# Five orders for the sixteen matmuls of a weight chunk, and one split buffer moved by 32 bytes

## The chip, the cores and the metric

The kernel runs on one core of a Trainium2 chip. The metric is the device time of one execution in microseconds. The engines named below are TensorE (PE, with its weight loads PEld), VectorE (DVE), ScalarE (ACT), GpSimd (POOL) and SyncE (SP), whose queue issues the loads of weights.

## What is computed

Two layers of a bidirectional encoder, on 256 positions of width 2048, in float32. The first layer mixes by multi-scale pooling and grouped-query attention, the second by an mLSTM with 8 heads of 256, and each ends in a gated MLP of width 5632 with a convolution over three positions:

```python
def reference(x, ...):
    for layer in range(DEPTH):
        h = rms_norm(x, norm_mix[layer])
        if layer % 2 == 0:
            proj = h @ w_in_ab[e]            # pooling | q | k | v
            ...
            mixed = jnp.concatenate([pool_out, att_out], axis=-1) @ w_out_ab[e]
        else:
            mixed = mlstm_mixer(h, w_in_c[o], b_gate_c[o], h_norm_c[o], w_out_c[o])
        x = x + mixed
        x = x + conv_ffn(rms_norm(x, norm_ffn[layer]), w_up[layer], conv_w[layer], conv_b[layer], w_down[layer])
    return x

def conv_ffn(x, w_up, conv_w, conv_b, w_down):
    u = x @ w_up
    ...
    gate, val = jnp.split(u, 2, axis=-1)
    return (jax.nn.silu(gate) * val) @ w_down
```

## The kernel before

Nearly all the work is products of activations with weights. Each float32 factor is split into a high half, rounded to the format that TensorE takes (`F32R`), and a low half, the rest; a product is then high by high, high by low and low by high.

**Weights.** They come in 818 chunks of 128 x 1024 floats, in one fixed order, through the class `Stream`. `load` issues the DMA of a chunk into a raw buffer `w`. `split` writes the high half with ScalarE (line 112) and the low half with VectorE (line 113) into one split buffer `hl` of shape 128 x 2 x 1024: `hl[:, 0]` is the high half, `hl[:, 1]` the low one. `next` hands TensorE the next chunk and runs loads and splits a few chunks ahead. There are four split buffers, in the pool `spool`; within a feed-forward layer `self.more` adds a fifth in a pool of its own (`fh0`, `fh1`), and `home` sends every chunk whose number leaves 4 when divided by 5 there.

**Two ways to multiply.** In `mov_part` and `mov_group` the activations are stationary and a chunk's weights stream past them, 512 columns to a matmul, 12 matmuls a chunk. (The tiles `dn`, `op`, `mo`, `mv`, `qproj`, `kproj`, `vproj`; the quads of the feed-forward layer, tile `p`, have 6 a chunk.) In `stat_part` the weights are stationary. A chunk then holds four row tiles (i = 0 to 3) of 128 rows by two column tiles (m = 0, 1), and each of its eight 128 x 128 blocks is loaded twice: the high block takes a matmul of 512 columns (high and low activations of 256 positions side by side, `src[:, 0:2, :]`), the low block one of 256 columns (high activations alone). These are the 16 matmuls of a chunk. They add up in PSUM: `ps[:, m]` is one bank, whose first half takes high by high and whose second half the two cross terms. `stat_group` uses it for `pool` in the attention layer and `mq`, `mk` in the mLSTM; `up` in the feed-forward layer calls `stat_part` for one chunk at a time, four to a tile f.

**Order.** TensorE's instructions stand in the order in which the program writes them (`manual_schedule`). `wv.tick` lets other work in between every four matmuls: transposes (`tr`, `xt`, `atr`), and attention products of 256 columns (`sc`, `ov`, `qk`, `av`). VectorE's and ScalarE's instructions are put in order by a scheduler that simulates the program. In the mLSTM, `head` transposes a matrix into `atr`, splits it into `at` (ScalarE line 819, VectorE line 820) and multiplies it (`av`); `scaled` evicts and scales `mq` and `mk`. In the feed-forward layer `gather` (lines 391 and 392) evicts an `up` tile, line 936 scales it by the row factors `R`, and `tail` does the rest. There are two PSUM tiles `mm` for the large products.

Of the kernel before, what the change touches and what calls it, by code (L numbers as in the profile page):

```python
# [10 lines left out]
F32R = mybir.dt.float32r  # L11
# [5 lines left out]
P = 128  # L17
D = 2048
S = 256
KT = D // P  # L20
# [9 lines left out]
MD = 256  # L30
# [3 lines left out]
CH = 8  # L34
# [27 lines left out]
NC_ML = M_BG + 1  # L62


class Stream:


# [38 lines left out]
    def split(self, then=None):  # L106
        i = self.n_split
        self.sums(i)
        w, n, width = self.w.pop(i)[:3]
        hl = self.home(i, False).tile([P, 2, CH * P], F32R, tag="hl", name=f"hl{i}")  # L110
        for c in range(0, width, n):
            (self.nc.vector.tensor_copy if i + c == 0 else self.nc.scalar.copy)(hl[:, 0, c : c + n], w[:, c : c + n])  # L112
            self.nc.vector.tensor_sub(hl[:, 1, c : c + n], w[:, c : c + n], hl[:, 0, c : c + n].bitcast(F32))  # L113
            then and then(c // n)
        self.hl[i] = hl
        self.n_split += 1
        self.sums(i + 1)
# [63 lines left out]
def trunk(ctx: ExitStack, tc: tile.TileContext, gx, xT, xn, call, catt, cml, weights, out):  # L181
    nc = tc.nc
    v, a, g, pe = nc.vector, nc.scalar, nc.gpsimd, nc.tensor
# [19 lines left out]
    st = Stream(tc, wp, sp, weights, 5, 2)  # L203
# [3 lines left out]
    first = ExitStack()  # L207
# [10 lines left out]
    wv = Weave()  # L218
# [7 lines left out]
    def mm(out_, lhsT, rhs, start, stop):  # L226
        pe.matmul(out_, lhsT, rhs, start=start, stop=stop, skip_group_check=True)  # L227
# [96 lines left out]
            v.tensor_copy(R, pr[:, 0:S])  # L324
            self.R = R

    def stat_group(act, kts, name):

        ps = mmp.tile([P, 2, 2, S], F32, tag="mm", name=name)
        stat_part(ps, act, kts, True, True)  # L330
        return ps

    def stat_part(ps, act, kts, first, last):

        n = len(kts)
        hl = None
        for i, k in enumerate(kts):
            if i % 4 == 0:
                hl = st.next()
            src = act(k)  # L340
            c = (i % 4) * 2 * P
            for m in range(2):
                mm(ps[:, m].rearrange("p a b -> p (a b)"), hl[:, 0, c + m * P : c + m * P + P],
                   src.rearrange("p a b -> p (a b)"), first and i == 0, False)
            for m in range(2):
                mm(ps[:, m, 1, :], hl[:, 1, c + m * P : c + m * P + P], src[:, 0, :], False,
                   last and i == n - 1)
            wv.tick(0.645)

    def mov_part(ps, act, kts, first, last):  # L350

# [36 lines left out]
    def gather(tp, ps, name):  # L388

        tb = tp.tile([P, 2, S], F32, tag="tb", name=f"tb_{name}")  # L390
        a.copy(tb, ps[:, :, 1, :])  # L391
        v.tensor_add(tb, ps[:, :, 0, :], tb)  # L392
        return tb

    def bc(ap, n):
        return ap.unsqueeze(1).to_broadcast([ap.shape[0], n, ap.shape[1]])
# [23 lines left out]
    def attention_layer(norm, nxt):  # L420
        with ExitStack() as es:
# [180 lines left out]
            def pool_group(ps, g2):  # L602
                if g2 == 0:
                    pw = tp.tile([P, 4, P], F32, tag="rot", name="pw")
                    a.dma_start(pw.rearrange("p g d -> p (g d)"), catt[:, A_PW : A_PW + 512])
                    inv = tp.tile([P, 4, S], F32, tag="rot", name="inv")
                    a.dma_start(inv.rearrange("p g d -> p (g d)"), catt[:, A_INV:])
                    pool_c.extend((pw, inv))
                pw, inv = pool_c
                u = gather(tp, ps, f"pool{g2}")  # L610
                v.tensor_mul(u, u, bc(norm.R, 2))
                yield 0.6
                pad = tp.tile([P, 2, S + 16], F32, tag="q0", name=f"pad{g2}")
                for j in range(2):
                    gi = 2 * g2 + j
                    w = WINDOWS[gi]

                    eng = (g, v)[j]
                    eng.memset(pad[:, j, 0:8], 0.0)
                    eng.memset(pad[:, j, 8 + S : S + 16], 0.0)  # L620
                    eng.tensor_copy(pad[:, j, 8 : 8 + S], u[:, j, :])
                    n, ln = 1, S + 16
                    cur = pad[:, j, :]
                    while n < w:
                        nx = t1p.tile([P, S + 16], F32, tag=(f"w{j}", f"qt2{j}")[n.bit_length() % 2],
                                      name=f"w{gi}_{n}")
                        ln -= n
                        eng.tensor_add(nx[:, :ln], cur[:, :ln], cur[:, n : n + ln])
                        cur, n = nx, 2 * n
                    o = 8 - w // 2  # L630
                    eng.tensor_mul(pad[:, j, :S], cur[:, o : o + S], inv[:, gi])
                    eng.tensor_sub(pad[:, j, :S], pad[:, j, :S], u[:, j, :])
                    yield 0.6
                yield 5.0
                py = psp.tile([P, 2, S], F32, tag="ps", name=f"py{g2}")
                for j in range(2):
                    mm(py[:, j, :], pw[:, 2 * g2 + j, :], pad[:, j, :S], True, True)
                for j in range(2):
                    c = cat(2 * g2 + j)
                    scale = cst[:, C_PSC + 2 * g2 + j : C_PSC + 2 * g2 + j + 1]  # L640
                    a.activation(c[:, 0, :], py[:, j, :], AF.Copy, scale=scale)
                    v.scalar_tensor_tensor(c[:, 1, :], py[:, j, :], scale, c[:, 0, :].bitcast(F32),
                                           ALU.mult, ALU.subtract)
                done.add(f"pool{g2}")
# [13 lines left out]
            ps = mov_group(xx, "kproj", 512, ahead, tables)  # L658
# [5 lines left out]
            with tc.manual_schedule(engines={mybir.EngineType.SP}):  # L664
                ps = mov_group(xx, "qproj0", after=squares)
            wv.add(q_block(ps, 0, 5.5))
            ps = mov_group(xx, "vproj")
# [12 lines left out]
                wv.add(q_block(mov_group(xx, f"qproj{qb}"), qb, (5.0, 4.5)[qb - 1]))  # L680
            pool_c = []
            for g2 in range(2):
                wv.add(pool_group(stat_group(xx, list(range(KT)), f"pool{g2}"), g2))
            need = [set(range(8)), {"pool0", "pool1"}, set(range(8, 12))]

            def ready(i):
# [5 lines left out]
    def mlstm_layer(norm, nxt):  # L692
        with ExitStack() as es:
# [69 lines left out]
            def scaled(ps, name, scale):  # L763
                u = gather(tp, ps, name)
                v.scalar_tensor_tensor(u, u, scale, bc(norm.R, 2), ALU.mult, ALU.mult)
                r = tp.tile([P, 2, 2, S], F32R, tag=name[0] + "hl", name=f"hl_{name}")
                a.copy(r[:, 0], u)
                v.tensor_sub(r[:, 1], u, r[:, 0].bitcast(F32))
                return r
# [3 lines left out]
            low = kc[:, M_MSK + P : M_MSK + 2 * P]  # L773
# [94 lines left out]
            for hp in range(MH // 2):  # L868
                vf = t1p.tile([P, 2, 512], F32, tag="vf", name=f"mvf{hp}")
                for c, n in ((0, MD + 32), (MD, MD)) if hp == 0 else ((0, 512),):  # L870
                    ps = mov_group(xx, f"mv{hp}_{c}", n)
                    if hp + c == 0:
                        wv.until(lambda: norm.rcol is not None)
                        wv.add(gates(ps))
                    n = min(n, 512 if hp else MD)
                    for t in range(2):
                        a.activation(vf[:, t, c : c + n], ps[:, t, :n], AF.Copy, scale=norm.rcol[:, t : t + 1])
                vt = t1p.tile([P, 2, 2, 512], F32R, tag="vt", name=f"mvt{hp}")
                a.copy(vt[:, 0], vf)
                v.tensor_sub(vt[:, 1], vf, vt[:, 0].bitcast(F32))  # L880
                if hp == 0:
                    nrcol = kp.tile([P, 2], F32, tag="nrcol", name="nrcol")
                    v.tensor_scalar_mul(nrcol, norm.rcol, -1.0)
                for hh in range(2):
                    h = 2 * hp + hh
                    q = scaled(stat_group(xx, list(range(KT)), f"mq{h}"), f"q{h}", MD ** -0.5)
                    kk = scaled(stat_group(xx, list(range(KT)), f"mk{h}"), f"k{h}", 1.0)
                    wv.add(head(h, q, kk, vt, hh))
                wv.add(gated(mov_group(xx, f"mo{hp}"), [2 * hp, 2 * hp + 1]))

# [6 lines left out]
    def ffn_layer(layer, norm, nxt):  # L897
        with ExitStack() as es:
# [29 lines left out]
            def up(f, gt, i):  # L928
                ps = mmp.tile([P, 2, 2, S], F32, tag="mm", name=f"up{layer}_{f}")
                for q in range(KT // 4):  # L930
                    stat_part(ps, xx, list(range(4 * q, 4 * q + 4)), q == 0, q == KT // 4 - 1)
                    if q < KT // 4 - 1:
                        yield
                wv.until(lambda: norm.R is not None)
                u = gather(tp, ps, f"up{layer}_{f}")
                v.tensor_mul(u, u, bc(norm.R, 2))  # L936
                tail(u, f, gt, i)
# [167 lines left out]
            for step in _ffn_plan():  # L1105
                kind, c = step[:2]
                if kind != "d" and c not in gts:
                    gts[c] = actp.tile([P, 8, 2, S], F32R, tag=f"B{c % 2}", name=f"g{layer}_{c}")
                key = step[:3]
# [251 lines left out]
```

## Time and profile before

| what | value |
|---|---|
| median of three runs | 2188.6 us (2188.59 to 2188.68) |
| the profiled execution | 2188.64 us |
| its span, first to last instruction | 2186.3 us |
| TensorE busy, matmuls | 2180.1 us, 11328 |
| VectorE busy | 1673.3 us |
| ScalarE busy | 1229.4 us |
| read from HBM | 436.74 MB, 201 GB/s over the span |

The time outside the span is 2.3 us. [...] How far two matmuls stand apart is seen in the chain of waits, which goes back from the last instruction and gives each piece of it by start, length and count.

### The profile page before, as it was taken

The page shows a single profiled execution, that of the slowest core. Times are in us where ns is not written, and L with a number is a line of the kernel's source. Part 1 is how long each engine was busy: PE and PEld are TensorE (multiplying, and loading weights), DVE is VectorE, ACT ScalarE, POOL GpSimd, SP SyncE. Part 2 cuts the span into 40 slices and gives each one's busy share as a digit, 9 for nine tenths or more (in the row PEclk, how much of TensorE's full clock was granted, in tenths as well). Part 3 has the DMA queues.
Part 4 walks back from the last instruction along what each step waited for, and adds up shares of the span by engine and source line. Part 5 has one row for each costly group of instructions (what it writes and reads, how often), then busy time and mean ns, then how long its engine had stood idle before and what let it go on. Part 6 is the DMA issues. An engine that isn't in the chain of part 4 may idle for free.

```text
span 2186.3 us, 30347 instructions
## 1 busy us (share of the span) xinstructions
PE 2180.1 (100%) x11328; PEld 1861.1 (85%) x11328; DVE 1673.3 (77%) x2378; ACT 1229.4 (56%) x1744; POOL 29.2 (1%) x40
## 2 busy tenths in 40 slices
PE   9999999999999999999999999999999999999999
PEld 7888888888888888889888888888888888888887
DVE  7686798878887786666767676679987888778664
ACT  7665565656555565556555554556565655556552
POOL 0020000000000000000000000000000000000000
PEclk9999999999999999999999999999999999999999
DMA  9555557675676755557565555655677667676563
GB/s 323 181 168 174 183 186 231 229 230 195 229 226 221 226 195 192 186 161 205 160 202 179 181 179 176 196 183 181 233 231 226 198 220 233 221 222 196 193 189 125
DMA packets 124950, 440.88 MB, mean 202 GB/s; under 512 B 13850, under 2 KB 16194, under 8 KB 124802
## 3 DMA queue, kind: packets, MB, share of 16 engines
q1 hardware_dynamic: 121568, 434.93, 61.4%
q10 hardware_dynamic: 3074, 3.75, 0.8%
q8 instruction: 89, 1.46, 0.3%
q14 instruction: 59, 0.48, 0.1%
q0 software_dynamic: 160, 0.26, 0.0%
HBM read 436.74 MB, written 2.14 MB: 201 GB/s over the span
## 4 chain that ended last, share of the span: by engine, by line
PE 97%; DVE 2%; issue 0%; ACT 0%
PE up L227 34%; PE dn L227 21%; PE op L227 8%; PE p L227 7%; PE mv L227 4%; PE mq L227 4%; PE mk L227 4%; PE mo L227 4%; PE qproj L227 3%; PE pool L227 1%; PE kproj L227 1%; PE vproj L227 1%; DVE hl L113 1%; PE av L227 1%; PE qk L227 1%; PE end L227 0%
## 5 line engine op out<-in xcount | busy, mean ns | idle before, releaser
L113 DVE TENSOR_TENSOR hl<-w,hl 128x1024 fp32r<-128x1024 f32 (+1 forms) x820 | 992.6, 1218 | 357.6 <-ACT hl L112 350.8
L112 ACT CAST hl<-w 128x1024 fp32r<-128x1024 f32 (+1 forms) x819 | 852.4, 1048 | 662.1 <-PE up L227 137.3
L227 PE MATMUL up<-xx,hl 128*128 128x512 f32 (+1 forms) x4608 | 823.1, 337 | 0.0
L227 PEld LDWEIGHTS up<-xx,hl 128*128 128x128 f32 x4608 | 716.1, 188 | 109.1
L227 PE MATMUL dn<-hl,g 128*128 128x512 f32 x2064 | 480.9, 390 | 0.0
L227 PEld LDWEIGHTS dn<-hl,g 128*128 128x128 f32 x2064 | 385.0, 188 | 78.5
L227 PE MATMUL p<-hl,sx 128*128 128x512 f32 x384 | 103.5, 391 | 1.1 <-DVE hl L113 1.1
L391 ACT COPY tb_up<-up 128x512 f32<-128x512 f32 x72 | 42.2, 587 | 99.4 <-PE up L227 94.8
L917 ACT ACTIVATE y<-tb_up,cst 128x256 f32<-128x256 f32 x144 | 78.8, 595 | 32.6 <-DVE tb_up L936 30.4
L227 PE MATMUL mk<-xx,hl 128*128 128x512 f32 (+1 forms) x512 | 92.2, 338 | 0.0
L227 PE MATMUL mq<-xx,hl 128*128 128x512 f32 (+1 forms) x512 | 92.2, 337 | 0.0
L227 PE MATMUL mv<-hl,xx 128*128 128x512 f32 (+2 forms) x480 | 91.7, 350 | 0.0
L227 PE MATMUL op<-hl,cat 128*128 128x512 f32 x384 | 91.6, 393 | 0.0
L227 PE MATMUL mo<-hl,xx 128*128 128x512 f32 x384 | 90.5, 391 | 0.0
L227 PE MATMUL op<-hl,mcat 128*128 128x512 f32 x384 | 89.5, 392 | 0.0
L227 PEld LDWEIGHTS mq<-xx,hl 128*128 128x128 f32 x512 | 79.3, 188 | 11.6
L227 PEld LDWEIGHTS mk<-xx,hl 128*128 128x128 f32 x512 | 79.1, 188 | 11.4
L227 PEld LDWEIGHTS mv<-hl,xx 128*128 128x128 f32 x480 | 78.3, 189 | 11.2
L392 DVE TENSOR_TENSOR tb_up<-up,tb_up 128x512 f32<-128x512 f32 x72 | 49.8, 692 | 47.7 <-ACT tb_up L391 47.6
L227 PEld LDWEIGHTS op<-hl,mcat 128*128 128x128 f32 x384 | 71.5, 188 | 14.6
L227 PEld LDWEIGHTS mo<-hl,xx 128*128 128x128 f32 x384 | 71.0, 188 | 14.3
L227 PEld LDWEIGHTS op<-hl,cat 128*128 128x128 f32 x384 | 70.9, 188 | 14.1
(240 smaller groups left out, 1740.2 us busy)
## 6 DMA issues: line engine op xcount, KB each, us to landing
w<-in_up SPq DMA_DIRECT2D x288, 512.0 KB, 4.2
w<-in_dn SPq DMA_DIRECT2D x176, 512.0 KB, 4.2
w<-in_m_in SPq DMA_DIRECT2D x124, 512.0 KB, 4.1
w<-in_q SPq DMA_DIRECT2D x112, 512.0 KB, 4.0
w<-in_a_in SPq DMA_DIRECT2D x46, 512.0 KB, 4.4
w<-in_a_out SPq DMA_DIRECT2D x32, 512.0 KB, 3.4
w<-in_m_out SPq DMA_DIRECT2D x32, 512.0 KB, 3.4
w<-in_m_g SPq DMA_DIRECT2D x5, 432.0 KB, 3.5
```

Of the source, the lines that this page charges most:

```text
L112: (self.nc.vector.tensor_copy if i + c == 0 else self.nc.scalar.copy)(hl[:, 0, c : c + n], w[:, c : c + n])
L113: self.nc.vector.tensor_sub(hl[:, 1, c : c + n], w[:, c : c + n], hl[:, 0, c : c + n].bitcast(F32))
L227: pe.matmul(out_, lhsT, rhs, start=start, stop=stop, skip_group_check=True)
L391: a.copy(tb, ps[:, :, 1, :])
L392: v.tensor_add(tb, ps[:, :, 0, :], tb)
L917: a.activation(y[:, j, :], u[:, j, :], AF.Identity, scale=cw(tl, 1), bias=cw(tl, 3))
```

## The change

In `stat_part` the 16 matmuls of a chunk are taken from a table, `ORDERS`, of five orders; in each triple i is the row tile, m the column tile and `low` the half. A caller names the order. Order 0 takes two row tiles at a time, their four high blocks and then their four low ones. Order 1 takes all eight high blocks, row tile by row tile, and then all eight low ones. Order 2 does so too, but goes through the four row tiles of one column tile before the other. Order 3 takes column tile 0, four high and four low, and then column tile 1. Order 4 is that of before: per row tile two high and two low. `pool` has order 3; `mq` and `mk` have 2 and 3 in turn; `up` has f modulo 5. `wv.tick` still comes after every fourth matmul. In `split`, the fifth buffer's tile is 64 floats longer, and the chunk begins 8 floats (32 bytes) into it.

```diff
+def _orders():
+
+    one = [(i, m, low) for i in range(4) for low in range(2) for m in range(2)]
+    return [sorted(one, key=key) for key in (
+        lambda e: (e[0] // 2, e[2]), lambda e: e[2], lambda e: (e[2], e[1]), lambda e: (e[1], e[2]))] + [one]
+
+
+ORDERS = _orders()
...
-        hl = self.home(i, False).tile([P, 2, CH * P], F32R, tag="hl", name=f"hl{i}")
+        home = self.home(i, False)
+        if home is self.spool:
+            hl = home.tile([P, 2, CH * P], F32R, tag="hl", name=f"hl{i}")
+        else:
+            hl = home.tile([P, 2 * CH * P + 64], F32R, tag="hl", name=f"hl{i}")
+            hl = hl[:, 8 : 8 + 2 * CH * P].rearrange("p (a b) -> p a b", a=2)
...
-    def stat_part(ps, act, kts, first, last):
+    def stat_part(ps, act, kts, first, last, order):
...
-        for i, k in enumerate(kts):
-            if i % 4 == 0:
-                hl = st.next()
-            src = act(k)
-            c = (i % 4) * 2 * P
-            for m in range(2):
-                mm(ps[:, m].rearrange("p a b -> p (a b)"), hl[:, 0, c + m * P : c + m * P + P],
-                   src.rearrange("p a b -> p (a b)"), first and i == 0, False)
-            for m in range(2):
-                mm(ps[:, m, 1, :], hl[:, 1, c + m * P : c + m * P + P], src[:, 0, :], False,
-                   last and i == n - 1)
-            wv.tick(0.645)
+        for c in range(0, n, 4):
+            hl = st.next()
+            src = [act(k) for k in kts[c : c + 4]]
+            for at, (i, m, low) in enumerate(ORDERS[order]):
+                w = hl[:, low, (2 * i + m) * P : (2 * i + m + 1) * P]
+                if low:
+                    mm(ps[:, m, 1, :], w, src[i][:, 0, :], False, last and c + i == n - 1)
+                else:
+                    mm(ps[:, m].rearrange("p a b -> p (a b)"), w, src[i].rearrange("p a b -> p (a b)"),
+                       first and c + i == 0, False)
+                if at % 4 == 3:
+                    wv.tick(0.645)
...
-                wv.add(pool_group(stat_group(xx, list(range(KT)), f"pool{g2}"), g2))
+                wv.add(pool_group(stat_group(xx, list(range(KT)), f"pool{g2}", 3), g2))
...
-                    q = scaled(stat_group(xx, list(range(KT)), f"mq{h}"), f"q{h}", MD ** -0.5)
-                    kk = scaled(stat_group(xx, list(range(KT)), f"mk{h}"), f"k{h}", 1.0)
+                    q = scaled(stat_group(xx, list(range(KT)), f"mq{h}", 2 + h % 2), f"q{h}", MD ** -0.5)
+                    kk = scaled(stat_group(xx, list(range(KT)), f"mk{h}", 3 - h % 2), f"k{h}", 1.0)
...
-                    stat_part(ps, xx, list(range(4 * q, 4 * q + 4)), q == 0, q == KT // 4 - 1)
+                    stat_part(ps, xx, list(range(4 * q, 4 * q + 4)), q == 0, q == KT // 4 - 1, f % len(ORDERS))
```

How the instructions move is shown at two places. The first is TensorE in the mLSTM, head 0, from the last chunk of `mq` (`hl_8945`) into the first chunk of `mk` (`hl_8966`); each row is an instruction's line, operation, output and inputs, the size of its output and how often it stands there in succession. 128x512 are high blocks, 128x256 low ones; `cols` is a small product that a tick lets in. Before:

```order
L227 MATMUL mq_8921<-xx_2399,hl_8945 128x512 x2
L227 MATMUL mq_8921<-xx_2399,hl_8945 128x256 x2
L227 MATMUL cols<-cst,rows_b 128x40 x4
L227 MATMUL mq_8921<-xx_2399,hl_8945 128x512 x2
L227 MATMUL mq_8921<-xx_2399,hl_8945 128x256 x2
L227 MATMUL mk_9027<-xx_2399,hl_8966 128x512 x2
L227 MATMUL mk_9027<-xx_2399,hl_8966 128x256 x2
```

and with the change:

```order
L242 MATMUL mq_8921<-xx_2399,hl_8945 128x512 x8
L242 MATMUL mq_8921<-xx_2399,hl_8945 128x256 x4
L242 MATMUL cols<-cst,rows_b 128x40 x4
L242 MATMUL mq_8921<-xx_2399,hl_8945 128x256 x4
L242 MATMUL mk_9027<-xx_2399,hl_8966 128x512 x4
L242 MATMUL mk_9027<-xx_2399,hl_8966 128x256 x4
```

The pairs of two long and two short matmuls have become eight and eight in `mq` (order 2) and four and four in `mk` (order 3).

The second place is VectorE in the mLSTM, head 0, where `at` is split for the product `av`; `tb_q` is the evicted `mq` of the next head, `A` and `arg` are the head's matrices, `hl` the split of weights. Before:

```order
L788 SCALAR_TENSOR_TENSOR arg_9390<-G_9387,mc,kml 128x128
L392 TENSOR_TENSOR tb_q_9240<-mq_9119,tb_q_9240 128x512
L113 TENSOR_TENSOR hl_9279<-w_9171,hl_9279 128x1024
L820 TENSOR_TENSOR at_9266<-atr_9261,at_9266 128x512
L765 SCALAR_TENSOR_TENSOR tb_q_9240<-tb_q_9240,R_8741 128x512
```

and with the change:

```order
L802 SCALAR_TENSOR_TENSOR arg_9390<-G_9387,mc,kml 128x128
L406 TENSOR_TENSOR tb_q_9240<-mq_9119,tb_q_9240 128x512
L128 TENSOR_TENSOR hl_9279<-w_9171,hl_9279 128x1024
L779 SCALAR_TENSOR_TENSOR tb_q_9240<-tb_q_9240,R_8741 128x512
L834 TENSOR_TENSOR at_9266<-atr_9261,at_9266 128x512
```

`at` now stands behind the scaling of `tb_q`; the same holds for heads 2, 4 and 6. On ScalarE, `at`'s high half (`CAST at<-atr`) stands behind the exponential `ACTIVATE arg<-arg` at the same four places, where it stood ahead of it. Beyond that the scheduler swaps neighbours in a few places, among them `COPY R<-npr`, which goes behind one split of weights at the start of each feed-forward layer. The order of the loads on SP is the same.

More of the change, by code (lines that the diff above doesn't have):

```diff
@@ L325, in finish, with stat_group @@
             self.R = R
-    def stat_group(act, kts, name):
+    def stat_group(act, kts, name, order):
         ps = mmp.tile([P, 2, 2, S], F32, tag="mm", name=name)
-        stat_part(ps, act, kts, True, True)
+        stat_part(ps, act, kts, True, True, order)
         return ps
-    def stat_part(ps, act, kts, first, last):
+    def stat_part(ps, act, kts, first, last, order):
         n = len(kts)
-        hl = None
-        for i, k in enumerate(kts):
-            if i % 4 == 0:
-                hl = st.next()
-            src = act(k)
-            c = (i % 4) * 2 * P
-            for m in range(2):
-                mm(ps[:, m].rearrange("p a b -> p (a b)"), hl[:, 0, c + m * P : c + m * P + P],
-                   src.rearrange("p a b -> p (a b)"), first and i == 0, False)
-            for m in range(2):
-                mm(ps[:, m, 1, :], hl[:, 1, c + m * P : c + m * P + P], src[:, 0, :], False,
-                   last and i == n - 1)
-            wv.tick(0.645)
+        for c in range(0, n, 4):
[10 more added lines that the diff above has]
+                    wv.tick(0.645)
     def mov_part(ps, act, kts, first, last):
```

## The prediction

> **What bounds the kernel now.** I read the page's span, engine table and shares of the chain first, then the view of the cores, then the waits of TensorE.
>
> ```profile
> span 2186.3 us, 30347 instructions
> PE 2180.1 (100%) x11328; PEld 1861.1 (85%) x11328; DVE 1673.3 (77%) x2378; ACT 1229.4 (56%) x1744; POOL 29.2 (1%) x40
> PE 97%; DVE 2%; issue 0%; ACT 0%
> core 0: 2186.3 us, clock 1.000
> PE wps L251 <- DVE pad L620: 1.2, 1, 1.2
> PE p L227 <- DVE hl L113: 1.1, 2, 0.5
> ```
>
> TensorE is busy all the span, the chain that ends last is 97% TensorE, the clock is granted in full, and the two waits listed for TensorE come to 2.3 us. So the time is the sum of the steps from one matmul to the next, and the change counts only if it alters those steps or makes TensorE wait. Since matmuls overlap, a mean duration (396 ns for 512 columns) is no step. The chain of waits in order of time gives steps, because it adds a piece's length from end to end:
>
> ```profile
> 802.57 22.28 PE up L227 x128
> 824.85 10.89 PE dn L227 x48
> 835.74 22.28 PE up L227 x128
> 2127.95 43.53 PE dn L227 x192
> ```
>
> An `up` piece is 8 chunks of 16 matmuls, so a chunk takes 22.28 / 8 = 2785 ns. A long run of 512-column matmuls steps at 43.53 / 192 = 226.7 ns. Runs of 256-column matmuls stand inside such streams where attention works:
>
> ```profile
> 121.69 0.71 PE sc L227 x6
> 122.40 4.11 PE qproj L227 x18
> 1064.29 1.43 PE qk L227 x12
> 1065.72 5.47 PE mo L227 x24
> 1075.76 1.43 PE av L227 x12
> 1077.19 4.11 PE mo L227 x18
> ```
>
> Twelve short ones less six are 1.43 - 0.71 = 0.72 us, 120.0 ns each; 24 long ones less 18 are 5.47 - 4.11 = 1.36 us, 226.7 ns each, as above. 256 columns more are thus 106.7 ns, and about 13.3 ns per matmul are fixed. Eight long and eight short ones without neighbours' effects would be 8 x 226.7 + 8 x 120.0 = 2773 ns. The chunk takes 12 ns more, and it goes from long to short and back four times: 3 ns for each such turn.
>
> **What a turn costs after a longer run.** The same rows say it. Six short and the 18 long behind them take 0.71 + 4.11 = 4.82 us against 0.72 + 4.08; twelve and 18 take 5.54 against 1.44 + 4.08; twelve and 24 take 6.90 against 1.44 + 5.44. Each is 20 ns over (rows round to 10 ns), all of it in the long ones behind the short run. So a turn with six or twelve short matmuls and many long ones costs 20 ns, where one with two and two costs 3. A longer run isn't cheaper because it turns less often.
>
> **The change, part by part.** No matmul, weight load or byte is added or removed; the stationary chunks' order changes.
>
> ```profile
> L227 PE MATMUL up<-xx,hl 128*128 128x512 f32 x2304 | 724.8, 396 | 0.0
> L227 PE MATMUL mk<-xx,hl 128*128 128x512 f32 x256 | 80.7, 397 | 0.0
> L227 PE MATMUL mq<-xx,hl 128*128 128x512 f32 x256 | 80.7, 397 | 0.0
> L227 PE MATMUL pool<-xx,hl 128*128 128x512 f32 x64 | 20.6, 404 | 0.0
> ```
>
> Eight long ones per chunk make 288 + 32 + 32 + 8 = 360 chunks. `up` takes its order from f mod 5, with f = 0-15, 20-31 and 36-43 in each of two layers: 64, 64, 56, 56 and 48 chunks for orders 0 to 4. `mq` and `mk` give 32 chunks to order 2 and 32 to order 3, `pool` 8 to order 3. Orders 0 and 3 make two turns of four and four (64 + 56 + 32 + 8 = 160 chunks), orders 1 and 2 one turn of eight and eight (64 + 56 + 32 = 152), and order 4 is the old one (48, no change).
>
> *Eight and eight.* Eight short ones lie between the six and the twelve of the rows: 20 ns a turn. One turn is 20 against 12 now: +8 ns, x 152 = +1.2 us.
>
> *Four and four.* No row shows this. Below, the 3 ns of two and two; above, the 20 ns of six and more. Four lies midway in count, which would be 11 to 12; I take 13, since six and twelve cost alike, so that the cost must rise early and then stand. Two turns are 26 against 12: +14 ns, x 160 = +2.2 us. At the bounds: 6 against 12 gives -1.0 us, 40 against 12 gives +4.5 us.
>
> [...]
>
> *The low halves.* The splitting engines are ahead:
>
> ```profile
> 802.57:824.85 22.28, 22.28 (x129) 19.45 (x129) 14.95 (x20) 10.89 (x14) 0.00 (x0) 1.00 0.62 200
> 266.49:290.88 24.39, 24.39 (x142) 21.28 (x141) 23.49 (x35) 15.76 (x22) 0.00 (x0) 1.00 0.61 187
> ACT hl L112 <- PE up L227: 137.3, 115, 2.3
> ```
>
> The columns are length, then TensorE, weight loads, VectorE, ScalarE. VectorE works 14.95 of 22.28 us in a usual stretch, and ScalarE's splits wait for TensorE to free buffers. New orders want the low half later (fourth or eighth matmul in place of the second) and give the buffer back at the same sixteenth one: nothing. Only in the stretch from 266 us, where VectorE has 0.9 us to spare, could a late split show.
>
> *What the scheduler moved.* In the mLSTM `at` goes behind one ScalarE and one VectorE instruction, for the four even heads:
>
> ```profile
> 1044.93 0.59 ACT L819 CAST at<-atr 128x512 fp32r<-128x512 f32 x1 [0.29 <-PE atr L817]
> 1045.41 0.85 ACT L790 ACTIVATE arg<-arg 128x768 f32<-128x768 f32 x1
> 1046.11 0.69 DVE L820 TENSOR_TENSOR at<-atr,at 128x512 fp32r<-128x512 f32 x1
> 1046.71 0.68 DVE L765 SCALAR_TENSOR_TENSOR tb_q<-tb_q,R 128x512 f32<-128x512 f32 x1
> 1048.22 0.52 PE L227 MATMUL av<-mvt,at 128*128 128x256 f32 x3
> ```
>
> `at` is whole at 46.80 and wanted at 48.22: 1.42 us of cover. The exponential ahead of the cast uses ScalarE's 0.29 us of idling and delays it by about 0.56; VectorE puts the 0.68 us of `tb_q` ahead meanwhile. I expect `at` some 0.7 us later, so nothing; if 0.85 + 0.68 added up, 0.11 us a head, 0.4 us in all. `R` goes behind one split in each feed-forward layer, but the eviction that frees PSUM (L392) doesn't read it: nothing.
>
> *The 32 bytes.* The fifth home holds a fifth of the feed-forward chunks:
>
> ```profile
> L227 PE MATMUL up<-xx,hl 128*128 128x512 f32 (+1 forms) x4608 | 823.1, 337 | 0.0
> L227 PE MATMUL dn<-hl,g 128*128 128x512 f32 x2064 | 480.9, 390 | 0.0
> L227 PE MATMUL p<-hl,sx 128*128 128x512 f32 x384 | 103.5, 391 | 1.1 <-DVE hl L113 1.1
> L227 PE MATMUL p<-hl,xx 128*128 128x512 f32 x288 | 78.7, 390 | 0.0
> ```
>
> With the 48 of the end, (4608 + 2112 + 672) / 5 = 1478 matmuls read it. No row shows an operand moved by 32 bytes; the nearest is the 13.3 ns fixed part, which might double or vanish: 19.7 us either way. I take nothing, because the two `up` pieces above meet the five homes at different places and are equal to 10 ns. [...] A slower split there is covered by the windows above.
>
> *Sum.* 1.2 + 2.2 = +3.4 us (bounds of the turns: +0.2 and +5.7 us). The profiled execution took 2188.64 us, 2.3 us outside its span, and stands at the runs' median of 2188.6: 2192.0 us.
>
> **The rivals.**
>
> *Cheap turns (2186.3).* A turn costs 3 ns at any length: -6 x 160 - 9 x 152 = -2.3 us. For it: fewer turns, and the measured 3 ns. Against: 20 ns in three places.
>
> *Dear turns (2194.3).* Four short ones already cost 20 ns: +4.5 + 1.2 us. For it: twelve cost no more than six, so the cost is full early. Against: two cost 3.
>
> *The offset costs (about 2202; to 2212).* Loads or streams from the moved buffer take another 13.3 ns: half of 1478 x 13.3 = +9.9 us on the forecast, all +19.7. For it: the fixed part is unexplained. Against: nothing in the trace depends on place.
>
> *The offset gains (about 2179).* The other side: the 13.3 ns come from loads and streams meeting in memory, and the moved buffer avoids two thirds of them, 1478 x 9 = -13 us. It decides for "faster" from 5.3 ns a matmul, (3.4 + 4.4) / 1478. For it: the fixed part isn't column time. Against: short and long, weights as stationary or moving operand, show the same 13.3.
>
> *Order doesn't matter (2188.6).* The 20 ns belong to the attention products themselves, not to run length, and every chunk stays at 2785 ns. For it: all three places are inserted products. Against: the excess lies in the projection matmuls behind them.
>
> **How the numbers follow.** Forecast (turns of four between 10 and 16 ns or so, with waits of up to a microsecond) 0.38; cheap turns 0.10; dear turns 0.18; offset costs 0.17; offset gains 0.10; order doesn't matter 0.07. A measurement here can tell about 0.2%, 4.4 us, from no change. Slower by more (over 2193.0): dear turns, the offset's cost and 0.13 of the forecast, 0.48. Within: 0.25 of the forecast, 0.08 of cheap turns and 0.07, 0.40. Faster (under 2184.2): the offset's gain and 0.02 of cheap turns, 0.12. The range 2185.5 to 2202 leaves out the offset's gain and the upper half of its cost. The forecast's own range is 2190 to 2194.
>
> **What would show it.** In the chain of waits the `up` pieces of 128 (two f each, 22.28 us now) come to 22.34 with orders 1 and 2 or with order 4 beside 0 or 3, and to 22.37 with 0 and 1; `mk` and `mq` pieces of 64 follow by 0.03 to 0.06 us. Pieces under 22.26 mean cheap turns, over 22.39 dear ones. `dn` pieces of 48 stay at 10.89 us unless the offset counts: from 10.92 it costs, under 10.86 it gains. TensorE's waits stay near 2.3 us; a wait on `hl` or `at` of over a microsecond in total would make the prediction wrong in its reasons.

## The result, and the profile after

The changed kernel takes 2197.03 us (median of six runs, 2196.89 to 2197.17) against 2188.60 us for the kernel before in the same session (2188.47 to 2188.68): +8.4 us, a ratio of 1.0039 with a 95% interval of 1.0026 to 1.0052. The forecast was +3.4 us.

The page of the changed kernel begins with the span, the engines' busy times and, further down, the shares of the chain that ended last:

```profile
span 2194.6 us, 30349 instructions
PE 2188.7 (100%) x11328; PEld 1868.4 (85%) x11328; DVE 1673.6 (76%) x2378; ACT 1228.5 (56%) x1744; POOL 29.2 (1%) x40
PE 97%; DVE 2%; issue 0%; ACT 0%
```

The span grew by 8.3 us and TensorE's busy time by 8.6, with the same 11328 matmuls. VectorE and ScalarE are as busy as before. TensorE's waits, in the view of waits (who waits, at which line, for whom, total, count, longest):

```profile
PE wps L266 <- DVE pad L634: 1.2, 1, 1.2
PE p L242 <- DVE hl L128: 0.8, 2, 0.4
```

They come to 2.0 us, 2.3 before. So no new wait took the time: the steps from one matmul to the next are longer. Which ones, the chain of waits in order of time shows (start, length, piece, count):

```profile
788.85 5.61 PE up L242 x32
794.46 10.90 PE dn L242 x48
805.35 22.34 PE up L242 x128
827.69 11.03 PE dn L242 x48
838.72 22.34 PE up L242 x128
861.06 11.00 PE dn L242 x48
872.06 22.35 PE up L242 x128
894.41 10.99 PE dn L242 x48
905.40 22.42 PE up L242 x128
2135.79 43.91 PE dn L242 x192
2179.70 11.01 PE end L242 x48
```

The `up` pieces of 128 went from 22.28 to between 22.34 and 22.42 us. 22.34 to 22.37 was forecast; the slowest of the four is beyond 22.39, which the prediction gave as a mark of dear turns. But the `dn` pieces of 48, whose order was not touched, went from 10.89 to between 10.90 and 11.03, and the long one of 192 from 43.53 to 43.91. That is what the prediction named as the mark of an offset that costs. In the trace's single instructions the matmuls of `dn` that read the fifth split buffer step at 233.6 ns (the mean from the start of one to the start of the next), where those of the same chunks stepped at 226.8 before; in `p` and in the last chunks (`end`) the fifth buffer gives 233.5 too. Added up by tile from such steps, `up` takes 2.6 us more, `dn` 3.7, `p` 1.7 and `mq` with `mk` 0.5.

### The profile page after: what moved, and what is told of

Read it like the earlier page. It is cut to its first block, busy times and chain, and to the rows that moved or that the text cites. A ratio compares the mean times of both kernels' runs of the same rounds, so it can differ in the third digit from the quotient of the medians.

```text
span 2194.6 us, 30349 instructions
## 1 busy us (share of the span) xinstructions
PE 2188.7 (100%) x11328; PEld 1868.4 (85%) x11328; DVE 1673.6 (76%) x2378; ACT 1228.5 (56%) x1744; POOL 29.2 (1%) x40
## 4 chain that ended last, share of the span: by engine, by line
PE 97%; DVE 2%; issue 0%; ACT 0%
PE up L242 34%; PE dn L242 22%; PE op L242 8%; PE p L242 7%; PE mq L242 4%; PE mv L242 4%; PE mk L242 4%; PE mo L242 4%; PE qproj L242 3%; PE pool L242 1%; PE kproj L242 1%; PE vproj L242 1%; DVE hl L128 1%; PE av L242 1%; PE qk L242 1%; PE end L242 1%
## 5 line engine op out<-in xcount | busy, mean ns | idle before, releaser
L242 PE MATMUL mk<-xx,hl 128*128 128x256 f32 (+1 forms) x512 | 92.5, 338 | 0.0
```

## The experiments

Each kernel was timed beside the kernel before. The runs of one kernel lie within a few tenths of a microsecond of each other; the interval of a ratio is wider, near 0.001 on either side (2 us). "Piece" is an entry of the chain of waits, as above. Where no offset is named, the chunk lies at the start of the fifth buffer's tile, which stays 64 floats longer.

### One half of the change at a time

Orders alone:

```diff
-            hl = hl[:, 8 : 8 + 2 * CH * P].rearrange("p (a b) -> p a b", a=2)
+            hl = hl[:, 0 : 0 + 2 * CH * P].rearrange("p (a b) -> p a b", a=2)
```

> The five orders stay, the fifth buffer's chunk begins at its tile's start again. Theory (both parts cost, the offset more): the changed kernel's up, mq, mk and pool chunks with the orders alone are some 0 to 18 ns longer than 2785 ns, so +2 to +4 us, 2190.6 to 2192.6 us, and the dn pieces of 48 are back at 10.89 us. Rival (the orders make all of the 8.4 us, and dn is slower only because it follows them): 2197 us, dn pieces still at 11.0 us. Rival (the orders cost nothing): 2188.6 us.

Measured: 2192.40 us, ratio 1.0017 (1.0008 to 1.0026), +3.8 us. Its chain of waits at the same places:

```profile
803.90 22.32 PE up L242 x128
826.22 10.91 PE dn L242 x48
...
870.40 22.38 PE up L242 x128
...
2131.68 43.55 PE dn L242 x192
```

Offset alone (order 4 in all chunks, the chunk 8 floats in):

```diff
-            for at, (i, m, low) in enumerate(ORDERS[order]):
+            for at, (i, m, low) in enumerate(ORDERS[4]):
```

> All chunks go in the old order, the fifth buffer's chunk stays 32 bytes into its tile. Theory: every matmul that streams from the moved buffer takes some 7 ns more, so dn, end and p give +5 us, and up +1 us: 2193.5 to 2195 us, with dn pieces of 48 at about 10.97 us. Rival (orders alone): 2188.6 us, dn pieces at 10.89 us. Rival of the prediction (13.3 ns for each of 1478 matmuls): 2208 us.

Measured: 2195.11 us, ratio 1.0029 (1.0018 to 1.0041), +6.5 us.

```profile
804.89 22.35 PE up L242 x128
827.24 11.01 PE dn L242 x48
838.25 22.29 PE up L242 x128
...
2134.01 43.91 PE dn L242 x192
2177.91 11.01 PE end L242 x48
```

The orders leave the `dn` pieces almost where they were (10.91, 43.55) and lengthen `up` (22.32 to 22.38). The offset lengthens `dn` exactly as the whole change does (43.91; 11.01 at the end) and `up` less (22.29 to 22.35). Added up by tile, `dn` takes 0.5 us more with the orders and 3.6 with the offset, `up` 1.9 and 1.0. So the orders account for what was forecast, and the offset, taken as nothing, is the larger half. The two add to 10.3 us, and together they cost 8.4. The difference is no larger than the intervals of these ratios. By tile the missing 1.9 lie mostly in `p` (0.9 for the orders, 1.9 for the offset, 1.7 for both) and less in `dn` and `up`, 0.4 each. A step can be slowed by its neighbours or by its buffer, and I take it that it isn't slowed twice; that reading is argued, not shown.

### The price of a turn, by length of run

One order in all 360 stationary chunks, no offset. Four and four (order 3):

```diff
-            for at, (i, m, low) in enumerate(ORDERS[order]):
+            for at, (i, m, low) in enumerate(ORDERS[3]):
```

> No offset; all 360 stationary chunks take order 3 (four long, four short, twice). Forecast of the prediction, 14 ns a chunk: +5.0 us, 2193.6 us, up pieces of 128 at 22.39 us. Dear turns (28 ns a chunk): +10.1 us, 2198.7 us, pieces at 22.50 us. Cheap turns (-6 ns): 2186.4 us, pieces at 22.23 us.

Measured: 2195.41 us, ratio 1.0031 (1.0019 to 1.0042), +6.8 us, 19 ns a chunk where the forecast has 14.

```profile
805.24 22.43 PE up L242 x128
827.66 10.93 PE dn L242 x48
```

Eight and eight (`ORDERS[1]` in that line):

> No offset; all 360 stationary chunks take order 1 (eight long, eight short). Forecast of the prediction, 8 ns a chunk: +2.9 us, 2191.5 us, up pieces of 128 at 22.34 us. Cheap turns (-9 ns): 2185.4 us, pieces at 22.21 us. If a turn costs nothing at eight and eight beyond what two and two cost over the chunk: 2188.6 us.

Measured: 2190.11 us, ratio 1.0007 (0.9998 to 1.0016), +1.5 us, 4 ns a chunk where the forecast has 8. The interval reaches no change.

```profile
803.07 22.32 PE up L242 x128
825.39 10.91 PE dn L242 x48
```

Four and four in the other way, two row tiles over both PSUM banks in place of four row tiles in one (`ORDERS[0]`):

> No offset; all 360 stationary chunks take order 0: four long and four short as in order 3, but from one matmul to the next the PSUM bank changes. Theory (only the lengths of the runs count): as with order 3 alone, 2195.4 us and pieces of 128 at 22.43 us. Rival (matmuls that add into the same bank one after the other cost more): clearly less, 2192 us or so.

Measured: 2196.16 us, ratio 1.0034 (1.0022 to 1.0047), +7.6 us.

```profile
805.20 22.43 PE up L242 x128
827.62 10.93 PE dn L242 x48
```

The pieces are the same as with order 3, and the whole times lie 0.8 us apart, less than the intervals. The order of the banks plays no part that these runs show; the length of the run does. In both kernels the `dn` piece of 48 is at 10.93 us without any offset, above the 10.92 that the prediction took as the mark of the offset: this short piece feels its neighbours as well.

One and one, a sixth order that takes a high block and its own low block in turn:

```diff
-        lambda e: (e[0] // 2, e[2]), lambda e: e[2], lambda e: (e[2], e[1]), lambda e: (e[1], e[2]))] + [one]
+        lambda e: (e[0] // 2, e[2]), lambda e: e[2], lambda e: (e[2], e[1]), lambda e: (e[1], e[2]))] + [one, sorted(one, key=lambda e: (e[0], e[1]))]
...
-            for at, (i, m, low) in enumerate(ORDERS[order]):
+            for at, (i, m, low) in enumerate(ORDERS[5]):
```

> No offset; every stationary chunk goes one long, one short, block by block (eight turns a chunk). Theory (a turn costs the less the shorter the runs: 18 ns at four and four, 3 at two and two, nothing at one and one): 12 ns a chunk less, -4.3 us, 2184.3 us. Rival (a turn has 3 ns at least): 12 ns a chunk more, +4.3 us, 2192.9 us.

Measured: 2202.14 us, ratio 1.0062 (1.0049 to 1.0074), +13.5 us. Both numbers missed.

```profile
807.05 22.60 PE up L242 x128
```

Sixteen and sixteen: every other chunk runs backwards, so that the low blocks of two chunks stand together, then the high blocks of two. `mq`, `mk` and `pool` get the pattern too. The flag `last`, which `mm` takes as `stop`, goes to the last two matmuls of a group:

```diff
-            for at, (i, m, low) in enumerate(ORDERS[order]):
+            for at, (i, m, low) in enumerate(ORDERS[1][::-1] if (c // 4 + order) % 2 else ORDERS[1]):
...
```

> No offset; every other stationary chunk of a tile goes backwards (low halves first), so that the runs become sixteen long and sixteen short. Theory (a turn between long runs costs 20 ns, however long they are): half a turn a chunk, 2773 + 10 = 2783 ns, up pieces of 128 at 22.27 us and the whole 2188 us, at or below before. Rival (what costs is the number of long or short ones in a run, not the turn): at least 22.32 us a piece and 2190 us, as with eight and eight.

Measured: 2187.83 us beside 2188.54, ratio 0.9997 (0.9988 to 1.0006), -0.7 us.

```profile
802.41 22.27 PE up L242 x128
824.68 10.88 PE dn L242 x48
2127.01 43.52 PE dn L242 x192
```

The `up` piece is the one expected, 22.27 us. It is the fastest of the kernels run, but its interval includes no change.

From the pieces follows a table. A chunk without turns is taken at 2773 ns, as in the prediction; the rest is divided by the number of turns from long to short and back.

| run of | up piece of 128, us | per chunk, ns | turns | ns a turn |
|---|---|---|---|---|
| 1 | 22.60 | 2825 | 8 | 6.5 |
| 2 (before) | 22.28 | 2785 | 4 | 3 |
| 4 | 22.43 | 2804 | 2 | 15.4 |
| 8 | 22.32 | 2790 | 1 | 17 |
| 16 | 22.27 | 2784 | 1/2 | 21.5 |

From four on the price of a turn is high, 15.4 to 21.5 ns, and rises with the run. Pairs are the exception, and single ones are dearer than pairs (6.5 ns against 3). (A piece is rounded to 10 ns, which is about 1 ns a chunk.)

### Where the offset's cost comes from

Order 4 in all chunks, and the fifth buffer's chunk at other places in its tile. 64 bytes:

```diff
-            hl = hl[:, 8 : 8 + 2 * CH * P].rearrange("p (a b) -> p a b", a=2)
+            hl = hl[:, 16 : 16 + 2 * CH * P].rearrange("p (a b) -> p a b", a=2)
```

> The old order everywhere; the fifth buffer's chunk begins 64 bytes into its tile, not 32. Theory (what costs is a start that is no multiple of 64 bytes): 2188.6 us, dn pieces of 48 at 10.89 us. Rival (any shift of the fifth buffer against the other four costs): about 2195 us and dn pieces at 10.99 us, as with 32 bytes.

Measured: 2193.81 us, ratio 1.0024 (1.0015 to 1.0033), +5.2 us.

16 bytes (`hl[:, 4 : 4 + ...]`):

> The old order everywhere; the fifth buffer's chunk begins 16 bytes into its tile. Theory (a start that is no multiple of 64 bytes costs, by how many pieces of 64 bytes are touched): about 2195 us, as with 32 bytes. Rival (the cost grows with the shift): half of it, about 2192 us. [...]

Measured: 2194.71 us, ratio 1.0028 (1.0017 to 1.0038), +6.1 us.

128 bytes (`hl[:, 32 : 32 + ...]`):

> The old order everywhere; the fifth buffer's chunk begins 128 bytes into its tile. Theory (a start that is a multiple of 128 bytes is free; 16, 32 and 64 were not): 2188.6 us, the last dn piece of 192 at 43.53 us as before the change. Rival (any shift of the fifth buffer costs): about 2194 us and 43.9 us.

Measured: 2194.59 us beside 2188.54, ratio 1.0027 (1.0017 to 1.0038), +6.0 us. One row each of the chains of 64 bytes and of 128:

```profile
2132.75 43.83 PE dn L242 x192
```

```profile
2133.72 43.81 PE dn L242 x192
```

All four shifts cost 5 to 7 us, and their intervals overlap. Neither 64 nor 128 bytes came free (5.2 and 6.0 us). In the single instructions the fifth buffer's matmuls of `dn` step at 231.3, 233.6, 230.7 and 232.7 ns for 16, 32, 64 and 128 bytes.

The four split buffers of `spool` 32 bytes further, by a pad ahead of it. A second pad makes 128 bytes in all for the pools behind, the fifth buffer's among them if pools lie in the order in which the program opens them; its chunk is then 128 + 32 bytes further. The traces give no addresses.

```diff
+    pool("pad0", 1).tile([P, 8], F32, tag="pad0", name="pad0")
     sp = pool("wsplit", 4)
+    pool("pad1", 1).tile([P, 24], F32, tag="pad1", name="pad1")
```

> The old order everywhere; all five split buffers lie 32 bytes further on, the four of the pool too. Theory (each matmul that streams from a moved buffer pays about 6.8 ns): 2784 matmuls of dn, p and end and some 2100 of op, mo, mv and the q, k, v projections give +32 us, the 360 stationary chunks +3 to +5 us: 2223 to 2226 us. Rival (only the fifth buffer's place against the other four matters): 2188.6 us.

Measured: 2224.22 us, ratio 1.0162 (1.0147 to 1.0178), +35.6 us. The chain of waits of this kernel:

```profile
1016.34 7.01 PE mv L244 x60
2106.03 22.52 PE up L244 x128
2128.55 11.19 PE dn L244 x48
2162.25 44.81 PE dn L244 x192
2207.05 11.19 PE end L244 x48
```

Now all `dn` matmuls take the step that only the fifth buffer's had: 44.81 / 192 = 233.4 ns. The four buffers of `spool` follow each other as before and pay the same step; so it isn't that one buffer differs from the others, but where a buffer lies. And short ones of 256 columns got cheaper. The same piece of 256-column matmuls before was:

```profile
999.75 7.20 PE mv L227 x60
```

That is 120.0 ns a matmul before and 7.01 / 60 = 116.8 ns now. 512 columns cost 233.4, twice 116.8 within 0.2 ns, as if the step went with the columns alone, 0.456 ns each. A third length in the same run doesn't follow. These are matmuls of 288 columns, which would take 131.3 ns so and take 4.00 / 30 = 133.3 (132.0 before):

```profile
998.25 4.00 PE mv L244 x30
```

The 13.3 ns per matmul are thus not shown to be gone.

In the kernel before, the other operand, `xx`, 32 bytes further, with the split buffers at the starts of their tiles:

```diff
-            self.xx = actp.tile([P, KT, 2, S], F32R, tag="A", name=f"xx{n}")
+            xx = actp.tile([P, KT * 2 * S + 32], F32R, tag="A", name=f"xx{n}")
+            self.xx = xx[:, 8 : 8 + KT * 2 * S].rearrange("p (k a s) -> p k a s", k=KT, a=2)
```

> The kernel before, with the normalised activations xx 32 bytes further on and the split buffers where they were; xx streams in up, mq, mk and pool and is stationary in qproj, kproj, vproj, mv and mo. Theory (a stream that starts off a multiple of 128 bytes takes 233.3 and 116.8 ns in place of 226.7 and 120.0): a stationary chunk is 8 x 350.1 = 2801 ns, +16 ns, +5.6 us, 2194.2 us, and mo stays as it is. Rival (both operands count alike): mo pieces grow too, 2197 us or more.

Measured: 2222.21 us, ratio 1.0153 (1.0139 to 1.0167), +33.7 us. The theory's 2194.2 us missed; the rival's 2197 us or more came, but not for the rival's reason alone, as follows below. Its chain of waits:

```profile
803.91 11.16 PE dn L227 x48
815.07 22.50 PE up L227 x128
1015.16 7.20 PE mv L227 x60
2160.39 44.62 PE dn L227 x192
```

This run was less clean than its expectation says. By the order of the pools in the program, the longer tile of `xx` pushes everything behind it 128 bytes on, the four split buffers of `spool` among them. So `dn`, which doesn't read `xx` at all, met split buffers 128 bytes further than before, against a `g` that stayed (by the same order it stands ahead of `xx`): 44.62 / 192 = 232.4 ns, as a shift of 128 bytes gave the fifth buffer alone (232.7 ns in the single instructions). If the buffers lie so, the run shows that `up` pays when its operands are moved by different amounts (22.50 us, 22.28 before), and that 128 bytes of the four buffers cost nearly what 32 do of all five (44.62 us for the 192 of `dn`, 44.81 in e7). Its short matmuls of `mv` gained nothing: 7.20 / 60 = 120.0 ns, as before. It does not show what `xx` alone would do.

What stays open: the traces give no addresses, so how the operands lay before is not shown. Two readings fit these runs, and neither is shown: that each operand of a matmul has to lie on some multiple of more than 128 bytes to keep the step of 226.7 ns, or that the two operands have to lie alike to each other. A kernel that moves everything by 32 bytes together would tell them apart, and one that moves the fifth buffer by 256 bytes would show how coarse the grain is; neither was run.

## Why the prediction was right and where it failed

**What bounds the kernel.** TensorE's steps, and nothing else: the waits went from 2.3 to 2.0 us, VectorE's and ScalarE's busy times stayed within 1 us, and the time came from steps alone.

**The failed step: "The 32 bytes ... I take nothing".** That term of the sum was given 0 and measures +6.5 us alone (+4.6 beside the orders, 8.4 less 3.8). The reason given was that two `up` pieces meet the five homes at different places and are equal to 10 ns. This compares homes of which none was shifted; it could not bear on a shift of 32 bytes. The bound beside it, 19.7 us either way, held the cost: 6.5 us / 1478 = 4.4 ns. The rival "the offset costs" had the sign and the place, but its price, half or all of 13.3 ns per matmul, lies above that, and its mechanism, another 13.3 ns, was not what came: with all buffers moved (e7) 512 columns pay 6.7 ns more and 256 columns 3.2 ns less. So the products of long ones alone pay most: with all buffers shifted a chunk of `dn` pays 12 x 6.7 = 80 ns, one of `up`, half of it short, (22.52 - 22.28) / 8 = 30 ns. The steps next to a shifted chunk pay as well: in `dn` those of the four other buffers go from 227.3 to 227.9 ns on average when only the offset is changed.

The price hardly follows the size of the shift: 16, 32, 64 and 128 bytes cost 6.1, 6.5, 5.2 and 6.0 us (e6, e2, e5, e9).

**The orders.** "1.2 + 2.2 = +3.4 us" measures +3.8 (e1). That the sum is near is luck, since two errors offset each other. Four and four is dearer than forecast: 15.4 ns a turn and not 13, 19 ns a chunk and not 14. Eight and eight is cheaper: 17 ns and not 20, 5 ns a chunk and not 8 (the 20 ns were read from rows rounded to 10 ns). With these sizes the sum is 160 x 19 + 152 x 5 = 3.8 us. "Cheap turns" fell (pieces of 22.43 for four and four, where it gives 22.23). "Dear turns" gives four the 20 ns of the longer runs; 15.4 is nearer to the forecast's 13. "Order doesn't matter" fell with e3, and with it the view that the 20 ns belong to the attention products: plain stationary chunks show 15 to 21.5 ns.

**The work moved on other engines.** It cost nothing, as forecast. `at` in the mLSTM is split by VectorE at line 834 and multiplied into `av`; the view by tile gives count, durations (minimum, median, maximum) and first and last start:

```profile
L242 PE MATMUL av<-mvt,at x96: 277/283/284, 1052.5 to 1368.7; 128*128 128x256 f32 x96
L834 DVE TENSOR_TENSOR at<-atr,at x8: 684/684/687, 1050.7 to 1365.3; 128x512 fp32r<-128x512 f32 x8
```

In the first head it is whole at 1050.7 + 0.7 = 1051.4 us and wanted at 1052.5. Of the 1.42 us of cover 1.1 are left, more than the 0.7 expected. TensorE's waits name neither `at` nor a new wait on `hl` for the low halves.

**The chances.** Slower by over 0.2% had 0.48, and +0.39% came; that it came so clearly is the offset's doing. The orders alone measure +0.17%, within what was called the same. The forecast's own range, 2190 to 2194 us, was missed by 3 us. The wide range, 2185.5 to 2202, holds the 2197.03 only because it reached up to half of the rival's price for the offset; as far as the forecast's mechanism goes, that is luck.

## What to carry to other kernels

In this kernel, which is bound by TensorE's steps, the place of a matmul's operand in SBUF was part of its price: every shift tried, from 16 to 128 bytes, cost 512-column matmuls 2 to 3% (230.7 to 233.6 ns a step in place of 226.8), in one of five buffers or in all. So in a kernel bound the same way pads and odd tile lengths ahead of hot operands are worth looking for (a tile that is 32 floats longer went with `dn` matmuls that don't read it at 232.4 ns, 226.7 before). Where long and short matmuls alternate, count the turns and price them by run length from the profile: here pairs were cheapest per turn, 3 ns, and fours the worst trade of those from two up, 2804 ns a chunk against 2784 to 2790. A long piece of the chain of waits that the edit doesn't touch is a good witness for a side effect: the 192 matmuls of `dn` take 43.52 to 43.57 us with other orders alone and 43.91 with the offset, while the pieces of 48, which stand between `up` chunks, move with both.

## What the runs showed of the hardware that was not expected

Two ways of stepping showed. With the operands at their old places a long run of matmuls, each with its own weight load, steps at 226.7 ns (512 columns) and 120.0 ns (256): 106.7 ns for 256 columns and 13.3 ns fixed. With the split buffers 32 bytes further (e7) it steps at 233.4 and 116.8 ns, twice and once the same. How general the second way is stays open: 288 columns take 133.3 ns in e7, and in e12 long ones take 232.4 ns while 256 columns stay at 120.0.

Short runs bring the stream near to the second way without any shift, and single ones beyond it for 512 columns. From the single instructions of the `up` chunks that no other work interrupts (272 in each kernel), the mean from start to start:

| run of | kernel | 512 columns, ns | 256 columns, ns | sum, ns |
|---|---|---|---|---|
| 1 | e8 | 235.9 | 116.8 | 352.7 |
| 2 | before | 232.7 | 115.2 | 347.9 |
| 4 | e3 | 231.6 | 118.3 | 349.9 |
| 8 | e4 | 229.0 | 119.1 | 348.0 |
| 16 | e10 | 228.4 | 119.4 | 347.8 |

Pairs are cheap not because a turn costs them only 3 ns, as the prediction reads it, but because their short matmuls gain about what their long ones lose (115.2 ns against 120.0, 232.7 against 226.7). In fours the long ones still step slowly (231.6 ns) and the short ones have lost most of that gain (118.3 ns); 8 x (349.9 - 347.9) = 16 ns of the 19 ns a chunk of e3 are that. So the prediction's price per turn is a sum that fits, and not a mechanism. Why a turn or a shift should bring such steps about isn't shown by any run.
